# Two rows of the last tile stored so that one DMA engine gets less: half by SyncE, half by GpSimd on 15 engines

## The chip, the cores and the metric

The kernel runs on one core of a Trainium2 chip. The metric is the time of one execution in microseconds (us). All runs here are in the fast state or, where a run stands alone, of unknown state, with a granted clock of 1.0 in each. The effects are below 0.1%, so runs are compared only with runs of the kernel before from the same chip.

## The reference

```python
z = x + residual                                   # 32 x 2048 rows of 2048 float32
rms = np.sqrt(np.mean(z ** 2, axis=-1, keepdims=True) + eps)
return (z / rms * gamma).astype(np.float32)
```

Two arrays of 537 MB are read and one is written. There is nothing to reuse.

## The kernel before

The rows are cut into tiles of 128 partitions with 7 rows each (the first two tiles are smaller). SyncE loads x and stores the result, ScalarE issues the loads of the residual and computes the sums of squares, VectorE adds and scales in place in the buffer `z`. The last tile is handled in four pieces of 2, 2, 2 and 1 rows, so that its stores can start early:

```python
tail = [(0, 2), (2, 4), (4, 6), (6, 7)]
...
# SyncE, after the stores of all other tiles
for k, (a, b) in enumerate(tail):
    sp.wait_ge(tail_ev["done"], k + 1)             # VectorE has scaled piece k
    sp.dma_start(
        out=rows(o_f, last)[:, a:b, :], in_=z[last % 2][:, a:b, :]
    ).then_inc(s_tail, U)                          # U = 16: one increment per DMA engine
...
# GpSimd takes no part but for the waits at the end
nc.gpsimd.wait_ge(s_tail, U * len(tail))
nc.gpsimd.sem_clear(range(ids[0], ids[-1] + 1))
```

One row of one partition is 8 KB, so one row of a tile is 1 MB. In the trace the four stores of the tail land 16 times each (64 landings), with 384 packets of 16 KB and 128 of 8 KB. Dealt alike to the 16 DMA engines this is 8 partitions of each store, 24 packets of 611 ns and 8 of 309 ns, 17.1 us of work.

Of the kernel before, what the change touches and what calls it, by code (L numbers as in the profile page):

```python
# [9 lines left out]
def kernel(  # L10
# [5 lines left out]
    eps: float,  # L16
    out: bass.AP,
):



# [6 lines left out]
    nc = tc.nc  # L28
    P = nc.NUM_PARTITIONS
# [4 lines left out]
    x_f = x.flatten_outer_dims()  # L34
    r_f = residual.flatten_outer_dims()
    o_f = out.flatten_outer_dims()
# [4 lines left out]
    U = 16  # L41
# [8 lines left out]
    last = n_tiles - 1  # L50

    LO = 3
    n_iter = (last - LO) // 2
    HI = LO + 2 * n_iter
    assert n_iter >= 1

    def rows(t, i):
        k = sizes[i]
        return t[starts[i] : starts[i] + P * k, :].rearrange("(p r) m -> p r m", r=k)
# [5 lines left out]
    def sb(name, shape):  # L65
        return ctx.enter_context(nc.sbuf_tensor(name, shape, fp32))
# [6 lines left out]
    def sem(name):  # L73
        sems.append(ctx.enter_context(nc.semaphore(name)))
        return sems[-1]
# [3 lines left out]
    z = [sb(f"z{p}", [P, R, D]) for p in range(2)]  # L79
# [2 lines left out]
    ssq = [[sb(f"ssq{p}{h}", [P, 4]) for h in range(2)] for p in range(2)]  # L82
    rms = [[sb(f"rms{p}{h}", [P, 4]) for h in range(2)] for p in range(2)]
    rstd = [[sb(f"rstd{p}{h}", [P, 4]) for h in range(2)] for p in range(2)]
    tail_ssq = sb("tail_ssq", [P, R])
    tail_rms = sb("tail_rms", [P, R])
    tail_rstd = sb("tail_rstd", [P, R])
# [8 lines left out]
    dve = sem("dve_own")  # L96
    act = sem("act_own")
    s_tail = sem("s_tail")
    tail_ev = {k: sem(f"tail_{k}") for k in ("add", "rms", "done")}


    tail = [(0, 2), (2, 4), (4, 6), (6, 7)]
# [30 lines left out]
    def load_x(sp, t, d=0):  # L133
        i = t.i + d
        inc(sp.dma_start(out=z[i % 2][:, : sizes[i], :], in_=rows(x_f, i)), "x_in", i)

    def load_r(sp, t, d=0):
        i = t.i + d
        e = entry(i)
        inc(  # L140
            sp.dma_start(  # L141
                out=r_area[:, e : e + sizes[i], :],
                in_=rows(r_f, i) if t.it is None else r_full[t.it + (i - 2)],
            ),
            "r_in",
            i,
        )

    def sp_turn(sp, t):
        i = t.i  # L150
        t.wait(sp, "done", -1)
        inc(
            sp.dma_start(out=rows(o_f, i - 1), in_=z[(i - 1) % 2][:, : sizes[i - 1], :]),
            "s_out",
            i - 1,
        )
        if i == last:
            return
        t.wait(sp, "s_out", -1)
        if i + 1 == last:  # L160
            for k, (a, b) in enumerate(tail):
                sp.dma_start(  # L162
                    out=z[last % 2][:, a:b, :], in_=rows(x_f, last)[:, a:b, :]
                ).then_inc(x_tail[k], U)
        else:
            load_x(sp, t, 1)
# [50 lines left out]
    def act_part(s, chain, src, a, b, sq, rm):  # L217

        for g in range(a, b):
            if g > a:  # L220
                chain.wait()
            chain.next(
                s.activation(  # L223
                    out=sq_junk[:, :],
                    in_=src[:, g, :],
                    func=Act.Square,
                    accum_out=sq[:, g - a : g - a + 1],
                )
            )
        chain.wait()  # L230
        return s.activation(  # L231
            out=rm, in_=sq[:, : b - a], func=Act.Sqrt, bias=eps_tile[:, :], scale=inv_d
        )

    def act_turn(s, t, chain):
        i, p = t.i, t.p
        for h, (a, b) in enumerate(parts(i)):
            chain.wait()
            t.wait(s, "add_a" if h == 0 else "add_b")
            if h == 0 and i > 0:  # L240
                load_r(s, t, 1)
            inc(
                act_part(s, chain, z[p], a, b, ssq[p][h], rms[p][h][:, : b - a]),
                "rms_a" if h == 0 else "rms_b",
                i,
            )
# [6 lines left out]
    def sync_program(sp):  # L253
        load_x(sp, Turn(0))
        load_r(sp, Turn(0))

        sp.wait_ge(tail_ev["add"], 1)
        for q in range(4):
            sp.dma_start(  # L259
                out=stage[32 * q : 32 * q + 1],  # L260
                in_=gamma.partition_broadcast(1).rearrange("p (a b) -> p a b", a=16),
            ).then_inc(g_in, U)
        load_r(sp, Turn(1))
        load_x(sp, Turn(1))
        for i in range(1, n_tiles):
            sp_turn(sp, Turn(i))
        for k, (a, b) in enumerate(tail):
            sp.wait_ge(tail_ev["done"], k + 1)
            sp.dma_start(
                out=rows(o_f, last)[:, a:b, :], in_=z[last % 2][:, a:b, :]  # L270
            ).then_inc(s_tail, U)

    def vector_program(v):
        v.memset(eps_tile[:, :], float(eps))  # L274
        v.memset(stage, 0.0).then_inc(tail_ev["add"], 1)  # L275
        v.wait_ge(g_in, 4 * U)
        v.stream_shuffle(gamma_tile[:, :].rearrange("p (a b) -> p a b", a=16), stage, [0] * 32)  # L277
        for i in range(LO):
            dve_turn(v, Turn(i), lambda i, h: (2 * i + h + 1) * U)
        with v.Fori(0, 2 * n_iter, 2) as it:  # L280
            for i in range(LO, LO + 2):
                dve_turn(v, Turn(i, it), lambda i, h: it * (2 * U) + (2 * i + h + 1) * U)
        for i in range(HI, last):
            dve_turn(v, Turn(i), lambda i, h: (2 * i + h + 1) * U)
        base = 2 * last * U
        t = Turn(last)
        t.wait(v, "r_in")

        def tail_scale(k):
            a, b = tail[k]  # L290
            v.wait_ge(tail_ev["rms"], k + 1)
            v.reciprocal(out=tail_rstd[:, a:b], in_=tail_rms[:, a:b]).then_inc(dve, U)  # L292
            v.wait_ge(dve, base + (k + 1) * U)
            scale(v, last, a, b, tail_rstd, a).then_inc(tail_ev["done"], 1)

        for k, (a, b) in enumerate(tail):
            v.wait_ge(x_tail[k], U)
            add(v, last, a, b).then_inc(tail_ev["add"], 1)
            if k:
                tail_scale(k - 1)  # L300
        tail_scale(len(tail) - 1)

    def scalar_program(s):
        chain = Chain(s, act)
        for i in range(LO):
            act_turn(s, Turn(i), chain)
        with s.Fori(0, 2 * (n_iter - 1), 2) as it:
            n = chain.n
            chain.base = it * R
            for i in range(LO, LO + 2):  # L310
                act_turn(s, Turn(i, it), chain)
            assert chain.n - n == 2 * R
        chain.base = None
        chain.n = n + 2 * R * (n_iter - 1)
        for i in range(HI - 2, last):
            act_turn(s, Turn(i), chain)
        for k, (a, b) in enumerate(tail):
            chain.wait()
            s.wait_ge(tail_ev["add"], k + 2)
            act_part(  # L320
                s, chain, z[last % 2], a, b, tail_ssq[:, a:b], tail_rms[:, a:b]
            ).then_inc(tail_ev["rms"], 1)

    sync_program(nc.sync)
    vector_program(nc.vector)
    scalar_program(nc.scalar)

    nc.gpsimd.wait_ge(ev["s_out"][(last - 1) % 2], ((last - 1) // 2 + 1) * U)
    nc.gpsimd.wait_ge(s_tail, U * len(tail))
    ids = [a.num for a in sems]  # L330
    assert ids == list(range(ids[0], ids[0] + len(ids)))
    nc.gpsimd.sem_clear(range(ids[0], ids[-1] + 1))
# [35 lines left out]
```

## Time and profile before

| | |
|---|---|
| time, median of 4 runs | 3724.88 us (3724.73 to 3724.96) |
| moved | 1610.68 MB at 433 GB/s |
| busy VectorE, ScalarE, GpSimd | 62%, 29%, 0% of the span |
| VectorE's last instruction ends | 3708.8 us |
| last landing of a store | 3722.59 us |

The prediction shows the end of the run in windows. Of the same view, these are the two windows ahead of those; the columns are the window, its length, the busy time of VectorE, ScalarE and GpSimd with their instructions, the granted clock, the mean busy share of the 16 DMA engines, and the rate in GB/s.

```profile
3690.00:3700.00 10.00, 9.96 (x6) 4.42 (x6) 0.00 (x0) 1.00 0.94 406
3700.00:3710.00 10.00, 8.73 (x6) 2.30 (x3) 0.00 (x0) 1.00 0.98 418
```

### The profile page before, as it was taken

How to read it: one execution, taken by the hardware profiler on the slowest of the kernel's cores; microseconds unless marked ns; L12 is line 12 of the kernel's file. 1: busy time of each engine (PE TensorE's matmuls, PEld its weight loads, DVE VectorE, ACT ScalarE, POOL GpSimd, SP SyncE). 2: the span in 40 equal slices, each digit the busy share in tenths (PEclk: the TensorE clock that was granted, in tenths of full speed). 3: DMA queues.
4: the chain of work that ended last, by engine and by line, in shares of the span. 5: the costliest groups of instructions: out<-in, count | busy, mean ns of one | idle time of the engine just before them, and what ended most of it. 6: DMA issues, size and time to landing. Idle time of an engine off the chain costs nothing.

```text
span 3723.7 us, 3798 instructions
## 1 busy us (share of the span) xinstructions
DVE 2302.6 (62%) x816; ACT 1072.4 (29%) x1176; POOL 0.2 (0%) x4
## 2 busy tenths in 40 slices
DVE  5666665566665566665566665566665566665566
ACT  2233322233322233322233322233322233322233
POOL 0000000000000000000000000000000000000000
DMA  9999999999999999999999999999999999999999
GB/s 421 431 434 435 434 434 435 434 435 435 434 434 434 434 434 434 434 434 433 434 434 434 434 434 434 434 434 434 434 434 434 434 434 434 434 434 434 434 432 398
DMA packets 32963, 1610.68 MB, mean 433 GB/s; under 512 B 3712, under 2 KB 3776, under 8 KB 3776
## 3 DMA queue, kind: packets, MB, share of 16 engines
q1 hardware_dynamic: 22592, 1082.17, 67.2%
q10 hardware_dynamic: 10368, 528.49, 32.8%
q14 instruction: 3, 0.02, 0.0%
HBM read 1073.77 MB, written 536.87 MB: 433 GB/s over the span
## 4 chain that ended last, share of the span: by engine, by line
DMA 67%; DVE 22%; issue 9%; ACT 2%; SPq 0%; DVEq 0%; ACTq 0%
DMA out_dram<-z 39%; DMA z<-in_x_dram 27%; DVE z L172 15%; DVE z L177 7%; ACT sq_junk L223 1%; ACT rms L231 0%; DVE rstd L197 0%; SPq L259 0%; DVEq L127 0%; DVE r_area L275 0%; ACTq L211 0%; ACTq L127 0%; SPq L141 0%; DVE tail_rstd L292 0%; SPq L162 0%
## 5 line engine op out<-in xcount | busy, mean ns | idle before, releaser
L172 DVE TENSOR_TENSOR z<-z,r_area 128x8192 f32<-128x8192 f32 (+2 forms) x150 | 1109.5, 7437 | 1252.5 <-DMA z<-in_x_dram 1252.5
L223 ACT ACTIVATE sq_junk<-z 128x2048 f32<-128x2048 f32 x512 | 963.4, 1882 | 2617.1 <-DVE z L172 2605.7
L177 DVE SCALAR_TENSOR_TENSOR z<-z,rstd,gamma_tile 128x2048 f32<-128x2048 f32 x505 | 1153.6, 2344 | 5.2
L197 DVE RECIPROCAL rstd<-rms 128x4 f32<-128x4 f32 (+2 forms) x146 | 25.3, 173 | 130.8 <-ACT rms L231 130.8
L223 ACT ACTIVATION_READ_ACCUMULATOR sq_junk<-z 128x1 f32 x512 | 95.5, 186 | 0.0
L231 ACT ACTIVATE rms<-ssq,eps_tile 128x4 f32<-128x4 f32 (+2 forms) x146 | 43.3, 297 | 13.4
L177 DVE SCALAR_TENSOR_TENSOR z<-z,tail_rstd,gamma_tile 128x2048 f32<-128x2048 f32 x7 | 16.2, 2345 | 0.1
L277 DVE LOAD_MASK_SELECT gamma_tile<-r_area x1 | 0.0, 14 | 16.1 <-DMA r_area<-in_gamma_dram 16.1
L277 DVE STREAM_SHUFFLE gamma_tile<-r_area 128x2048 f32<-128x2048 f32 x1 | 2.3, 2290 | 0.0
L275 DVE MEMSET r_area<- 128x2048 f32 x1 | 1.8, 1765 | 0.4 <-issue 0.4
L223 ACT ACT_TABLE_LOAD x1 | 1.3, 1283 | 0.9 <-SPq L77 0.9
L231 ACT ACT_TABLE_LOAD x1 | 1.3, 1283 | 0.1
L231 ACT ACTIVATE tail_rms<-tail_ssq,eps_tile 128x2 f32<-128x2 f32 (+1 forms) x4 | 1.2, 295 | 0.1
L274 DVE MEMSET eps_tile<- 128x1 f32 x1 | 0.1, 59 | 1.0 <-SPq L77 1.0
L292 DVE RECIPROCAL tail_rstd<-tail_rms 128x2 f32<-128x2 f32 (+1 forms) x4 | 0.6, 158 | 0.0
L349 POOL MEMSET const-bfloat16-1.0<- 128x1 bf16 x1 | 0.1, 101 | 0.0
L349 POOL MEMSET const-uint8-127<- 128x1 uint8 x1 | 0.1, 101 | 0.0
L349 POOL MEMSET const-float32-0.0<- 128x1 f32 x1 | 0.1, 98 | 0.2 <-issue 0.2
L349 POOL MEMSET const-float32-1.0<- 128x1 f32 x1 | 0.1, 98 | 0.0
## 6 DMA issues: line engine op xcount, KB each, us to landing
r_area<-in_residual_dram ACTq DMA_DIRECT2D x72, 7168.0 KB, 35.5
z<-in_x_dram SPq DMA_DIRECT2D x71, 7168.0 KB, 27.5
out_dram<-z SPq DMA_DIRECT2D x71, 7168.0 KB, 40.8
z<-in_x_dram SPq DMA_DIRECT2D x3, 2048.0 KB, 17.9
out_dram<-z SPq DMA_DIRECT2D x3, 2048.0 KB, 15.0
r_area<-in_residual_dram SPq DMA_DIRECT2D x1, 5120.0 KB, 25.0
z<-in_x_dram SPq DMA_DIRECT2D x1, 5120.0 KB, 36.7
out_dram<-z SPq DMA_DIRECT2D x1, 5120.0 KB, 26.5
```

Source lines behind the costliest of these rows:

```text
L172: return v.tensor_add(out=s, in0=s, in1=r_area[:, e + a : e + b, :])
L177: ins = v.scalar_tensor_tensor(out=s, in0=s, scalar=rs[:, c + g - a : c + g - a + 1], in1=gamma_tile[:, :], op0=mult, op1=mult,)
L197: v.reciprocal(out=rstd[p][h][:, :n], in_=rms[p][h][:, :n]).then_inc(dve, U)
L223: s.activation(out=sq_junk[:, :], in_=src[:, g, :], func=Act.Square, accum_out=sq[:, g - a : g - a + 1],)
L231: return s.activation(out=rm, in_=sq[:, : b - a], func=Act.Sqrt, bias=eps_tile[:, :], scale=inv_d)
L274: v.memset(eps_tile[:, :], float(eps))
L275: v.memset(stage, 0.0).then_inc(tail_ev["add"], 1)
L277: v.stream_shuffle(gamma_tile[:, :].rearrange("p (a b) -> p a b", a=16), stage, [0] * 32)
L292: v.reciprocal(out=tail_rstd[:, a:b], in_=tail_rms[:, a:b]).then_inc(dve, U)
L349: nc = _bacc.Bacc("TRN2", target_bir_lowering=False, num_devices=1)
```

## The change

The intent is to take work from one DMA engine in the last tile. It is called the fifth, because f1 finds it in a probe load of 5 partitions and not in one of 4; the four engines of the probe of 4 are called the first four. Rows 1 and 3 leave the full stores. SyncE stores their even partitions (64), GpSimd 60 of the odd ones, and SyncE the last 4. Two tiny loads on GpSimd, of 5 and of 12 partitions, stand before and behind its store.

```diff
-        for k, (a, b) in enumerate(tail):
+        for k, (a, b) in enumerate([(0, 1), (2, 3), (4, 6), (6, 7)]):
             sp.wait_ge(tail_ev["done"], k + 1)
-            sp.dma_start(
-                out=rows(o_f, last)[:, a:b, :], in_=z[last % 2][:, a:b, :]
-            ).then_inc(s_tail, U)
+            store_last(sp, slice(0, P), slice(a, b)).then_inc(s_tail, U)
+            if k == 1:
+                store_last(sp, slice(0, P, 2), slice(1, 4, 2)).then_inc(s_tail, U)
+                store_last(sp, slice(121, P, 2), slice(1, 4, 2)).then_inc(s_tail, U)
...
+    def pool_program(g):
...
+        turn(5, 0)                                  # tiny load of 5 partitions
+        g.wait_ge(tail_ev["done"], 2)
+        store_last(g, slice(1, 120, 2), slice(1, 4, 2)).then_inc(soft[2], U)
+        turn(12, 16)                                # tiny load of 12 partitions
+        for k in soft:
+            g.wait_ge(k, U)
+        g.dma_reset(range(soft[0].num, soft[-1].num + 1))
```

More of the change, by code (lines that the diff above doesn't have):

```diff
@@ L54 @@
     HI = LO + 2 * n_iter
-    assert n_iter >= 1
+    assert n_iter >= 1 and P == 128
     def rows(t, i):
@@ L84 @@
     rstd = [[sb(f"rstd{p}{h}", [P, 4]) for h in range(2)] for p in range(2)]
+    tiny = sb("tiny", [12, 32])
     tail_ssq = sb("tail_ssq", [P, R])
@@ L98 @@
     s_tail = sem("s_tail")
+    soft = [sem(f"soft{k}") for k in range(3)]
     tail_ev = {k: sem(f"tail_{k}") for k in ("add", "rms", "done")}
@@ L266, in sync_program, with store_last, turn, two_pairs @@
             sp_turn(sp, Turn(i))
-        for k, (a, b) in enumerate(tail):
+        for k, (a, b) in enumerate([(0, 1), (2, 3), (4, 6), (6, 7)]):
             sp.wait_ge(tail_ev["done"], k + 1)
-            sp.dma_start(
-                out=rows(o_f, last)[:, a:b, :], in_=z[last % 2][:, a:b, :]
-            ).then_inc(s_tail, U)
+            store_last(sp, slice(0, P), slice(a, b)).then_inc(s_tail, U)
+            if k == 1:
+                store_last(sp, slice(0, P, 2), slice(1, 4, 2)).then_inc(s_tail, U)
+                store_last(sp, slice(121, P, 2), slice(1, 4, 2)).then_inc(s_tail, U)
+    n_tail = 4 + 2
+    def store_last(eng, q, r):
+        return eng.dma_start(out=rows(o_f, last)[q, r, :], in_=z[last % 2][q, r, :])
+    def pool_program(g):
+        def turn(k, c):
+            def two_pairs(t):
+                return t[:k, c : c + 16].rearrange("p (a b) -> p a b", a=2)[:, :, :2]
+            g.dma_start(out=two_pairs(tiny), in_=two_pairs(x_f)).then_inc(soft[c // 16], U)
+        turn(5, 0)
[5 more added lines that the diff above has]
+        g.dma_reset(range(soft[0].num, soft[-1].num + 1))
     def vector_program(v):
@@ L326 @@
     scalar_program(nc.scalar)
+    pool_program(nc.gpsimd)
     nc.gpsimd.wait_ge(ev["s_out"][(last - 1) % 2], ((last - 1) // 2 + 1) * U)
-    nc.gpsimd.wait_ge(s_tail, U * len(tail))
+    nc.gpsimd.wait_ge(s_tail, U * n_tail)
     ids = [a.num for a in sems]
```

## The prediction

Passages of the recorded text that no trace or run of this case shows are cut, and the cuts marked: on what grounds a store runs on which engines, and the ground of rival 2, that the stores of the tail would run at a lower rate, with its worst case.

> **What bounds the kernel now.** I read the page first. VectorE is busy 62% and ScalarE 29% of the span, and no row of the page says that either of them is what the program waits for: the DMA row stands at 9 from the first slice to the last.
>
> ```profile
> span 3723.7 us, 3798 instructions
> DVE 2302.6 (62%) x816; ACT 1072.4 (29%) x1176; POOL 0.2 (0%) x4
> DMA  9999999999999999999999999999999999999999
> q1 hardware_dynamic: 22592, 1082.17, 67.2%
> q10 hardware_dynamic: 10368, 528.49, 32.8%
> HBM read 1073.77 MB, written 536.87 MB: 433 GB/s over the span
> ```
>
> The two queue shares add up to 100% of sixteen engines' time. The time is bytes over rate, 1610.68 MB at 433 GB/s, and the change moves no byte less. So nothing can be gained except where the sixteen engines are not all busy. The second view cuts the end of the run into windows; its last two columns are the mean busy share of the 16 DMA engines and the rate.
>
> ```profile
> 3710.00:3716.00 6.00, 0.00 (x0) 0.00 (x0) 0.00 (x0) 1.00 0.98 421
> 3716.00:3717.00 1.00, 0.00 (x0) 0.00 (x0) 0.00 (x0) 1.00 0.82 344
> 3717.00:3718.00 1.00, 0.00 (x0) 0.00 (x0) 0.00 (x0) 1.00 0.37 156
> 3718.00:3719.00 1.00, 0.00 (x0) 0.00 (x0) 0.00 (x0) 1.00 0.18 74
> 3719.00:3720.00 1.00, 0.00 (x0) 0.00 (x0) 0.00 (x0) 1.00 0.08 33
> 3720.00:3721.00 1.00, 0.00 (x0) 0.00 (x0) 0.00 (x0) 1.00 0.06 25
> 3721.00:3722.00 1.00, 0.00 (x0) 0.00 (x0) 0.00 (x0) 1.00 0.06 25
> ```
>
> A share of 0.06 is 1/16: from about 3719.7 us on a single engine is still storing. The raw landing times of the last store, one increment per engine, say the same: eleven engines at 3716.9 to 3717.9, four at 3718.8 to 3719.3, one at 3722.59; the span ends 1.15 us later. That straggler is also last in every earlier store of this tile, and its lag has grown over the run: the last load of the first part of the run spreads over 1 us, the late ones over 5 and more. It is one slow engine, not an accident of the tail.
>
> The third view is the timeline of the tail, with its column of the DMA-issuing queue (SPq). The four stores of the last tile are issued long before they land:
>
> ```profile
> 3690.41 18.76 SPq L269 DMA_DIRECT2D out_dram<-z  x4
> 3706.46 2.35 DVE L177 SCALAR_TENSOR_TENSOR z<-z,tail_rstd,gamma_tile 128x2048 f32<-128x2048 f32 x1
> ...
> out_dram<-z SPq DMA_DIRECT2D x3, 2048.0 KB, 15.0
> out_dram<-z SPq DMA_DIRECT2D x1, 1024.0 KB, 13.8
> ```
>
> A 2 MB store needs 4.8 us at 434 GB/s and takes 15 us to land, so it waits some 10 us behind older work in the engines' queues. VectorE ends at 3708.8 us, 14 us ahead of the last landing. In this tail neither computing nor issuing counts, only how many bytes each single engine still has to move.
>
> [...] Nothing in the kernel before uses GpSimd for a DMA or stores a part of the partitions[...].
>
> **The change part by part.** [...] So the diff wants the fifth engine relieved, and I take it that the author knows it to be the straggler. The kernel's trace names no engine; this is the assumption that I cannot check.
>
> Bytes per engine of the last tile: one row of 128 partitions is 8 partitions x 8 KB = 64 KB on each engine, seven rows 448 KB. Afterwards:
> - fifth engine: rows 0 and 2, 128 KB; its 4 of the 64 even partitions, rows 1 and 3, 64 KB; rows 4 and 5, 128 KB; row 6, 64 KB: 384 KB.
> - first four: 448 KB by the same sum with GpSimd's 4 partitions (64 KB), plus one of the partitions 121 to 127 each, two rows, 16 KB: 464 KB.
> - the other eleven: 448 KB.
>
> 384 + 4 x 464 + 11 x 448 = 7168 KB, the whole tile. Each engine moves 434 / 16 = 27.1 GB/s. The fifth loses 64 KB, 65,536 B / 27.1 GB/s = 2.42 us: landing at 3722.59 - 2.42 = 3720.2. In packets (309 ns for 8 KB, 611 ns for 16 KB in the trace) it is 24 x 611 + 8 x 309 before against 8 x 611 + 32 x 309 after, 2.36 us less. The first four gain 16 KB, 0.6 us; if they are the four that are late already, 3719.3 + 0.6 = 3719.9, still ahead of 3720.2. So the whole 2.4 us shows in the end.
>
> Costs: SyncE issues row 2, then two more stores at about 0.35 us each (the page's stores from L269 take 332 to 344 ns), after "done" at 3699.4. The engines then still hold older work: row 0 alone lasts until about 3702.4 (the first store landed at 3704.8, less the 2.4 us of the row that it no longer carries). The new stores have about 3 us to arrive, so I expect no gap. GpSimd's two 8-byte loads carry no bytes worth counting. Its reset waits for its own three transfers, which should land near 3711, 9 us ahead of the end. Three more semaphores are cleared in one range instruction. Sum: -2.4 us, with +0.5 us that I choose for packets of two queues, the finer pieces[...]: about -1.9.
>
> **The rivals.**
> 1. The relief goes to the wrong engine: [...] the straggler is not the fifth. Then it keeps its 448 KB and the end stays: 3724.9; with 464 KB, 3725.5. For it: [...] nothing here shows which engine lags. [...] About one in five.
> 2. [...] I expect a part of a microsecond; one in six that it eats the gain.
> 3. GpSimd's path becomes a new wait: slow descriptors, a late reset, or more work at start and end of the program for a third queue. Its slack of 9 us speaks against the first two; for the third I leave up to 1 us.
> 4. The main loop changes. No instruction in it does, and the 40 slices say that it is bound by bytes: excluded but for chance.
>
> **Range and chances.** Perfect levelling bounds the gain: the shares after 3716 us add up to 0.82 + 0.37 + 0.18 + 0.08 + 0.06 + 0.06 = 1.57 us of all sixteen, so the packets could end at 3717.6 instead of 3722.1, a gain of 4.5 us or 0.12% at the very most. Two per cent would be 74 us; neither side of it is within reach. Central value: 3724.93 - 1.9 = 3723.0. Low end: 3721.9, the full 2.4 and some luck at the ends. High end: 3725.8, rival 1 or a mild rival 2. The three runs before lie within 0.23 us, so the scatter does not widen this.
>
> **What the changed profile would show.** Right: a third queue with about 1 MB (60 x 2 x 8 KB = 983 KB), the last landing near 3720.2, the window 3721 to 3722 empty, four engines at about 3719 to 3720 and the span near 3721.5. Rival 1: the last two windows still at 0.06 until 3722. Rival 2: a DMA share or rate well under 0.98 and 420 GB/s between 3702 and 3712, with the bulk of the landings behind 3718. Rival 3: GpSimd's wait or reset ending after the last landing. The prediction is wrong if the end is above 3725.8, most likely by rival 2, or if a gap opens near 3702 because the smaller first store leaves the engines without work before the new ones arrive.

## More of the kernel before

A share counts how long packets were under way, the rate counts what they carried.

A packet is counted whole in the window in which it starts, so a share can pass 1.

## The result, and the profile after

| | median | runs |
|---|---|---|
| before | 3724.88 us | 3724.73 to 3724.96 (4) |
| changed | 3724.22 us | 3725.25, 3724.12, 3724.31, 3723.87 |

The ratio is 0.9999, with a 95% interval of 0.9981 to 1.0016. Ratios here are the mean time of one kernel's fast runs over that of the other's of the same rounds, so not quite the ratio of the medians. The interval is wider than anything that this change can do. The medians differ by 0.66 us. The profiled run, 3725.25, is the slowest of the four; the other three lie below all four runs before.

The queues and issues of the changed kernel, from its page and from the view of its DMA issues (queue: packets, MB, share; then size and us from issue to landing):

```profile
q0 software_dynamic: 208, 0.98, 0.1%
...
out_dram<-z POOLq DMA_DIRECT2D x1, 960.0 KB, 12.0
```

GpSimd's store is there as planned. GpSimd's timeline (start, duration, in us) shows that issuing it takes 0.65 us, and the store then has until the end of the run.

```profile
3700.45 0.65 POOL L282 DMA_DIRECT2D out_dram<-z  x1 [3698.18 <-DVE z L182]
3701.09 0.56 POOL L290 DMA_DIRECT2D tiny<-in_x_dram  x1
```

The windows of the changed kernel's end, to be set beside those of before:

```profile
3690.00:3700.00 10.00, 9.96 (x5) 5.10 (x8) 0.00 (x0) 1.00 0.96 414
3700.00:3710.00 10.00, 9.44 (x7) 2.30 (x3) 1.21 (x2) 1.00 0.98 353
3710.00:3716.00 6.00, 0.00 (x0) 0.00 (x0) 0.00 (x0) 1.00 1.00 395
3716.00:3717.00 1.00, 0.00 (x0) 0.00 (x0) 0.00 (x0) 1.00 1.03 434
3717.00:3718.00 1.00, 0.00 (x0) 0.00 (x0) 0.00 (x0) 1.00 0.91 385
3718.00:3719.00 1.00, 0.00 (x0) 0.00 (x0) 0.00 (x0) 1.00 0.53 221
3719.00:3720.00 1.00, 0.00 (x0) 0.00 (x0) 0.00 (x0) 1.00 0.33 139
3720.00:3721.00 1.00, 0.00 (x0) 0.00 (x0) 0.00 (x0) 1.00 0.25 106
3721.00:3722.00 1.00, 0.00 (x0) 0.00 (x0) 0.00 (x0) 1.00 0.08 33
```

Two things have changed. Between 3700 and 3710 us the share is 0.98 as before, but the rate is 353 GB/s where it was 418. That is 65 GB/s x 10 us = 0.65 MB not moved; the next six microseconds lose another (421 - 395) x 6 = 0.16 MB. Together, at 434 GB/s, this is 1.9 us of all 16 engines. And the end is no longer one engine alone: in the window from 3720 a share of 0.25 says that four are still at work, where it was 0.06 before. The last landing is at 3722.30 us.

The packet records say what the lost rate is. Before, every 8 KB packet of the tail takes 309 ns and none is longer. In the changed kernel the 120 packets of GpSimd's store take 411 ns in the mean and up to 1319, and SyncE's 8 KB packets 340 in the mean and up to 1431. I call this **stretch**: the time of each packet after 3690 us, less the shortest of its size and queue, summed. It is 30 us in this trace, which over 16 engines is again 1.9 us.

### The profile page after: what moved, and what is told of

Same layout as the page of the kernel before. It is cut to its first block, busy times and chain, and to the rows that moved or that the text cites. A ratio compares the mean times of both kernels' runs of the same rounds, so it can differ in the third digit from the quotient of the medians.

```text
span 3723.5 us, 3805 instructions
## 1 busy us (share of the span) xinstructions
DVE 2302.6 (62%) x816; ACT 1072.4 (29%) x1176; POOL 2.1 (0%) x7
## 4 chain that ended last, share of the span: by engine, by line
DMA 67%; DVE 22%; issue 9%; ACT 2%; SPq 0%; DVEq 0%; ACTq 0%
DMA out_dram<-z 39%; DMA z<-in_x_dram 27%; DVE z L177 15%; DVE z L182 7%; ACT sq_junk L228 1%; ACT rms L236 0%; DVE rstd L202 0%; SPq L264 0%; DVEq L132 0%; DVE r_area L302 0%; ACTq L216 0%; ACTq L132 0%; SPq L146 0%; DVE tail_rstd L319 0%; SPq L167 0%
## 5 line engine op out<-in xcount | busy, mean ns | idle before, releaser
L236 ACT ACTIVATE rms<-ssq,eps_tile 128x4 f32<-128x4 f32 (+2 forms) x146 | 43.3, 297 | 13.4
```

Source lines behind the costliest of these rows:

```text
L236: return s.activation(out=rm, in_=sq[:, : b - a], func=Act.Sqrt, bias=eps_tile[:, :], scale=inv_d)
```

## The experiments

Twelve kernels ran. In each group the kernel before ran on the same chip. Stretch is read from the packet records as above. All outputs were correct.

| run | median us (runs) | before, same chip | rate 3700 to 3710 | stretch, us |
|---|---|---|---|---|
| e1 halves by SyncE | 3724.97 (3724.75 to 3725.33) | 3724.97 | 416 | 0 |
| e2 full rows by SyncE | 3724.91 (3724.65 to 3725.10) | 3724.97 | 424 | 0 |
| e3 other engine left out | 3725.19 (3724.96 to 3725.46) | 3724.97 | 394 | 16 |
| e4 one row dealt anew | 3726.10 (3725.19 to 3726.37) | 3724.97 | 370 | 20 |
| f1 probes, before | 3725.19 (one) | 3725.25 | 426 | 0 |
| f2 probes, changed | 3724.72 (one) | 3725.25 | 369 | 23 |
| f3 full rows by GpSimd | 3725.23 (3724.89 to 3725.75) | 3725.25 | 423 | 0 |
| f4 half by GpSimd on 16 engines | 3725.02 (3724.97 to 3725.03) | 3725.25 | 424 | 0 |
| g1 odd partitions rotated | 3724.67 (3723.89 to 3726.27) | 3725.26 | 379 | 15 |
| g2 changed kernel again | 3724.67 (3724.43 to 3725.74) | 3725.26 | 385 | 13 |
| g3 tiny loads behind the store | 3725.66 (3725.55 to 3726.51) | 3725.26 | 385 | 15 |
| h1 row 0 in 19 stores | 3726.14 (3725.97 to 3726.81) | 3725.11 | 366 | 23 |

The kernel before ranged from 3724.63 to 3726.11 us over these four groups, within each group by 0.6 to 1.3 us. Differences of medians below half a microsecond are therefore not told as findings; the rate and the stretch are much clearer signs than the time.

**e1: are half stores the loss?** GpSimd is taken out. Theory A, in this and the next expectations, puts the loss on stores that deal a part of the partitions.

```diff
-                store_last(sp, slice(121, P, 2), slice(1, 4, 2)).then_inc(s_tail, U)
+                store_last(sp, slice(1, P, 2), slice(1, 4, 2)).then_inc(s_tail, U)
...
-    pool_program(nc.gpsimd)
```

> GpSimd is out of it: SyncE stores rows 1 and 3 as two halves, the 64 even partitions and then the 64 odd ones, over all 16 engines, so every engine has the 448 KB of the kernel before. Theory A [...]: the loss of the changed kernel stays without its relief, so 1.5 to 2.5 us slower than before, 3726.4 to 3727.4 us, and the rate between 3700 and 3710 us falls from 418 to some 350 GB/s as in the changed kernel. Theory B (the loss comes from GpSimd's third queue): 3724.9, rate 418. Theory C (the loss comes from finer pieces or from the smaller first store): 3725.5 to 3726.5, and the next run shows the same.

The rate stays and so does the time:

```profile
3700.00:3710.00 10.00, 7.86 (x6) 2.30 (x3) 0.00 (x0) 1.00 0.98 416
```

Theory A in this form is refuted: half stores through SyncE cost nothing here, 3724.97 us beside 3724.97. Every 8 KB packet takes 309 ns.

**e2: are small, late pieces or GpSimd's tiny loads the loss?**

```diff
-                store_last(sp, slice(0, P, 2), slice(1, 4, 2)).then_inc(s_tail, U)
-                store_last(sp, slice(121, P, 2), slice(1, 4, 2)).then_inc(s_tail, U)
+                store_last(sp, slice(0, P), slice(1, 4, 2)).then_inc(s_tail, U)
...
-        store_last(g, slice(1, 120, 2), slice(1, 4, 2)).then_inc(soft[2], U)
-        turn(12, 16)
+        turn(11, 16)
```

> Rows 1 and 3 are stored by SyncE for all 128 partitions in one store, so the pieces are as small (8 KB) and come as late as in the changed kernel, and GpSimd keeps its two tiny loads and its reset, but stores nothing. Theory A: [...] as before, 3724.6 to 3725.2 us and a rate near 418 between 3700 and 3710. Theory C or a cost of GpSimd's tiny loads and reset: 3725.5 or more.

3724.91 beside 3724.97, no stretch. The 8 KB pieces, the smaller first store, the tiny loads and the reset of GpSimd's state are all free here. No gap opened near 3702 us.

**e3: does it matter which engine is left out?**

```diff
-        turn(5, 0)
+        turn(12, 0)
...
-        turn(12, 16)
+        turn(5, 16)
```

> The two tiny loads change places, 12 partitions first and 5 last[...]. If [...] the fifth engine is the straggler, it loses its relief of 2.4 us and the time rises by that against the changed kernel: 3726.0 to 3727.0 us, with a single engine at a share of 0.06 for the last 2 us. If the relief of the fifth has no effect, 3724.2 as in the changed kernel[...].

3725.19, against 3724.97 before. The rise over the changed kernel was forecast as 1.8 us or more and is 1.0 against the first median and 0.5 against its second, and on other chips, so the size missed. The shape is near the expected one: one or two engines are left from 3719 us on, where the changed kernel had four from 3720 us on.

```profile
3719.00:3720.00 1.00, 0.00 (x0) 0.00 (x0) 0.00 (x0) 1.00 0.14 57
3720.00:3721.00 1.00, 0.00 (x0) 0.00 (x0) 0.00 (x0) 1.00 0.08 33
3721.00:3722.00 1.00, 0.00 (x0) 0.00 (x0) 0.00 (x0) 1.00 0.02 8
```

**e4: half of the bytes dealt anew.** GpSimd stores 120 partitions of row 0, SyncE the other 8 in two stores of 4.

```diff
-        for k, (a, b) in enumerate([(0, 1), (2, 3), (4, 6), (6, 7)]):
+        for k, (a, b) in enumerate([(1, 2), (2, 4), (4, 6), (6, 7)]):
...
-                store_last(sp, slice(0, P, 2), slice(1, 4, 2)).then_inc(s_tail, U)
-                store_last(sp, slice(121, P, 2), slice(1, 4, 2)).then_inc(s_tail, U)
+                store_last(sp, slice(120, 124), slice(0, 1)).then_inc(s_tail, U)
+                store_last(sp, slice(124, 128), slice(0, 1)).then_inc(s_tail, U)
...
-        g.wait_ge(tail_ev["done"], 2)
-        store_last(g, slice(1, 120, 2), slice(1, 4, 2)).then_inc(soft[2], U)
+        g.wait_ge(tail_ev["done"], 1)
+        store_last(g, slice(0, 120), slice(0, 1)).then_inc(soft[2], U)
```

The condition ahead of SyncE's two small stores also becomes `k == 0`.

> The same relief with half of the bytes dealt anew: only row 0 is taken out of the full stores, [...] rows 1 to 6 are full stores. Bytes per engine are as in the changed kernel (384, 464, 448 KB). Theory A: loss about in proportion to the bytes dealt anew, half of 1.8 us, so 3724.9 - 2.4 + 0.9 = 3723.4 us (3722.9 to 3723.9). Theory B or C: nothing gained over the changed kernel, 3724 to 3725.

A miss: 3726.10, slower than before in the median, with 20 us of stretch for half of the bytes. So the loss does not go by the bytes dealt anew. This store is issued 9 us earlier, while the previous tile's 56 KB packets are still in the queues, and four of those stretch too, one to 3.03 us where they take 2.12. The slowest engine lands the previous tile's store at 3707.7 us, in e1, e2 and e3 at 3704.7 to 3705.2.

The packet records show more: this run did not have "the same relief". The slowest engine's last two 56 KB packets, 3701.99 to 3704.11 and 3704.90 to 3707.02 us, have an 8 KB packet of GpSimd's queue between them and another behind, so this engine carried a part of GpSimd's store. The engine left out is one that was done with the previous tile at 3701.70 us. Why the store of 120 partitions was dealt so, no run shows. As a test of the time that theory A forecast, e4 is spoiled; its stretch still counts.

**f1 and f2: which engine is last?** Two tiny loads of 4 and 5 partitions stand behind the last store on SyncE's queue, with semaphores of their own.

```diff
+        for k in (4, 5):
+            sp.dma_start(
+                out=probe[:k, 32 * (k - 4) : 32 * (k - 4) + 16], in_=x_f[:k, :16]
+            ).then_inc(s_probe[k - 4], U)
```

> The kernel before with two probes behind its last store: tiny loads of 4 and of 5 partitions on SyncE, [...] each with its own semaphore, so that their landings tell when those engines have done their stores. If the fifth engine is the straggler, the probe of 5 has four landings before 3720 us and one near 3723, and the probe of 4 has none so late. If another engine lags, all nine landings are early. The time is as before or up to 1 us more.

> The changed kernel with the same two probes. Theory D (the fifth engine is relieved and the first four, which carry 16 KB more and are stretched, now end last): the four landings of the probe of 4 lie at 3721 to 3723 us, the fifth of the probe of 5 near 3720. Theory E (the relief did not reach the straggler): the fifth landing of the probe of 5 is the last of all, near 3722.

The landings of the probes, from the trace's semaphore records, in us (the first record of each probe, soon after its issue at 3709 to 3712 us, is left out):

```
before,  4 partitions: 3716.55 3717.68 3718.70 3719.38
before,  5 partitions: 3716.73 3717.85 3718.87 3719.57 3722.21
changed, 4 partitions: 3718.51 3718.82 3720.49 3721.30
changed, 5 partitions: 3718.69 3719.00 3720.67 3721.48 3721.75
```

The probe of 4 lands four times and that of 5 five times, taken here as one landing on each engine. Four landings of the second follow those of the first by 0.17 to 0.19 us; the last one, 3722.21 before, exists only in the probe of 5. By the names given above, **the fifth engine is the straggler**. Its lag has grown over the run: in f1 the last landing of a load came 0.2 us behind the second last at the start and 2.5 us at the end. Theory D and theory E each hold by half. In the changed kernel the fifth is still last, at 3721.75, but the slowest of the first four has come up to 0.3 us before it: it went from 3719.38 to 3721.30, 1.9 us, of which 16 KB would explain 0.6, if the store of 4 partitions runs on these four. The fifth engine's last stretch of work can be timed from its landing of the previous tile's store: 3704.96 to 3722.02 before, 17.06 us, and 3705.28 to 3721.55 with the change, 16.27. It moved 64 KB less, 2.4 us, and was faster by 0.8. By the packet times of the trace its work should take 17.1 us before, as it does, and 8 x 611 + 32 x 309 ns = 14.8 us with the change. So the fifth engine itself lost 1.5 us of its relief, and it began 0.3 us later. (One run of each kernel.)

**f3 and f4: is it GpSimd's queue?** In f3 GpSimd stores rows 1 and 3 of all partitions, in f4 the odd half on 16 engines. Theory A2 puts the stretch on GpSimd's store of 60 partitions, and theory B on any store through GpSimd's queue.

```diff
-        store_last(g, slice(1, 120, 2), slice(1, 4, 2)).then_inc(soft[2], U)
+        store_last(g, slice(0, P), slice(1, 4, 2)).then_inc(soft[0], U)       # f3
+        store_last(g, slice(1, P, 2), slice(1, 4, 2)).then_inc(soft[0], U)    # f4
```

In both the tiny loads and the 4-partition store are gone; f3 has no half store of SyncE either.

> GpSimd stores rows 1 and 3 of all 128 partitions in one store on all 16 engines, SyncE the other rows; no relief, no tiny loads. Theory A2 [...]: packets of 8 KB stay at 309 ns, time as before, 3724.7 to 3725.2. Theory B (any store through GpSimd's queue stretches packets, whatever the partitions): means of 365 to 410 ns as in the runs with a GpSimd store so far, time above 3725.5.

> As the run in which SyncE stored both halves, but the 64 odd partitions go through GpSimd, at the same time as the 64 even ones through SyncE, both on 16 engines. Theory A2: if both are dealt to the engines alike, [...] nothing stretches, 309 ns and 3724.7 to 3725.2 us; stretched packets here but not in the run with all 128 partitions would say that GpSimd deals 64 partitions in another way than SyncE. Theory B: stretched, above 3725.5.

The window of f3 and then of f4:

```profile
3700.00:3710.00 10.00, 8.49 (x6) 2.30 (x3) 0.32 (x1) 1.00 1.00 423
```

```profile
3700.00:3710.00 10.00, 8.07 (x6) 2.30 (x3) 0.00 (x0) 1.00 1.00 424
```

No packet is stretched in either. The stores through GpSimd's queue that run on all 16 engines cost nothing here, even beside one of SyncE's: 3725.23 us (f3) and 3725.02 (f4) beside 3725.25. Theory B is refuted.

**g1, g2, g3: is it the tiny load ahead of the store, or the split of the odd partitions?** g2 is the changed kernel again. g3 puts the tiny loads behind the store. g1 splits the odd partitions in another way: GpSimd stores the last 44, SyncE the first 20 in five stores of 4.

```diff
 # g1
-                store_last(sp, slice(121, P, 2), slice(1, 4, 2)).then_inc(s_tail, U)
+                for m in range(4):
+                    store_last(sp, slice(1 + 2 * m, 32, 8), slice(1, 4, 2)).then_inc(s_tail, U)
+                store_last(sp, slice(33, 40, 2), slice(1, 4, 2)).then_inc(s_tail, U)
...
-        store_last(g, slice(1, 120, 2), slice(1, 4, 2)).then_inc(soft[2], U)
-        turn(12, 16)
+        store_last(g, slice(41, P, 2), slice(1, 4, 2)).then_inc(soft[1], U)
```

```diff
 # g3
-        turn(5, 0)
         g.wait_ge(tail_ev["done"], 2)
         store_last(g, slice(1, 120, 2), slice(1, 4, 2)).then_inc(soft[2], U)
+        turn(5, 0)
         turn(12, 16)
```

> The same relief of the fifth engine (384, 464 and 448 KB as in the changed kernel), but the odd partitions of rows 1 and 3 are dealt[...]: GpSimd stores partitions 41 to 127, 44 in number[...], and SyncE stores the other 20 in five stores of 4 partitions[...]. Theory A2 [...]: packets of 8 KB stay near 309 ns, the fifth engine needs 2.4 us less from its previous landing to its last (14.7 in place of 17.1 us), the time is about 2 us below before, 3722.5 to 3723.3. Theory F (15 or fewer engines through GpSimd stretch in any case[...]): stretched as in the changed kernel, 3724 to 3725.

> The changed kernel again, unchanged, on the chip of these runs: 0.3 to 1.0 us below before, with 20 to 30 us of stretch summed over its 8 KB packets. It gives the scatter of the changed kernel beside the others.

> The changed kernel with both tiny loads behind the store[...]; no relief for the fifth. Theory A2: [...] no stretch (309 ns), and the time is that of before, within 0.4 us. Theory F: stretched as in the changed kernel, and as the fifth has its full 448 KB, 1 to 2 us above before.

Theory A2 forecast packets of 309 ns for g1 and g3. It misses in both: g3, without a tiny load ahead of the store, has 15 us of stretch, and g1 is stretched by 15 us and as fast as the changed kernel. Which engine takes which partitions, on which A2 rested, no run shows. The three windows, g1, g2 and g3:

```profile
3700.00:3710.00 10.00, 7.99 (x6) 2.30 (x3) 0.00 (x0) 1.00 0.96 379
```

```profile
3700.00:3710.00 10.00, 8.04 (x6) 2.30 (x3) 0.27 (x1) 1.00 0.97 385
```

```profile
3700.00:3710.00 10.00, 8.57 (x6) 2.30 (x3) 1.47 (x3) 1.00 0.98 385
```

g2 has less stretch than expected, 13 us. Its median lies 0.6 us below before, as in the first group (0.7) and in f2 (0.5, one run). g3 beside g2 is the cleanest measure of the relief: the same stores and stretch within 2 us, one with the fifth engine left out and one without. The medians are 3724.67 and 3725.66, **1.0 us for the relief**. All four runs of g3 lie above all nine of before, but its median is only 0.4 us higher, less than is told as a finding here.

**h1: row 0 in 19 stores.** Row 0 is cut into ten stores of SyncE and nine of GpSimd. Theory G forecast that this cut would avoid the stretch; its ground, an assumed dealing of partitions to engines, is not shown by any run.

```diff
-        for k, (a, b) in enumerate([(0, 1), (2, 3), (4, 6), (6, 7)]):
+        for k, (a, b) in enumerate([(1, 2), (2, 4), (4, 6), (6, 7)]):
...
+            if k == 0:
+                for m in range(4):
+                    store_last(sp, slice(m, 16, 4), slice(0, 1)).then_inc(s_tail, U)
+                    store_last(sp, slice(32 + m, 48, 4), slice(0, 1)).then_inc(s_tail, U)
+                store_last(sp, slice(16, 20), slice(0, 1)).then_inc(s_tail, U)
+                store_last(sp, slice(48, 52), slice(0, 1)).then_inc(s_tail, U)
...
+        store_last(g, slice(52, 96), slice(0, 1)).then_inc(soft[5], U)
+        for m in range(4):
+            turn(5, 16 * (m + 1))
+            store_last(g, slice(20 + m, 32, 4), slice(0, 1)).then_inc(soft[6 + 2 * m], U)
+            store_last(g, slice(96 + m, P, 4), slice(0, 1)).then_inc(soft[7 + 2 * m], U)
```

> The same relief (384 KB on the fifth engine, 464 on the first four, 448 on the others), by row 0 alone, cut into stores[...]. Theory G [...]: stretch summed over the packets under 3 us (13 to 30 us in the changed kernel), the fifth engine needs 14.7 us from its previous landing to its last, the time is 1.8 to 2.4 us below before. Theory F (stores on fewer than 16 engines through GpSimd stretch packets[...]): 10 us of stretch or more, and a time like that of the run that dealt row 0 in order, at or above before.

A clear miss for theory G: 3726.14, all five runs above all nine of before, and 23 us of stretch. Theory F's forecast came true: 10 us or more, and a time like e4's 3726.10. But h1 issues its row as early as e4 and in 19 stores, so more than the dealing differs from the changed kernel. GpSimd's own packets are hardly stretched (2.6 us in 88), but SyncE's of 8 and 16 KB are, by 8 and 11 us. At the end some five engines are left, not one:

```profile
3720.00:3721.00 1.00, 0.00 (x0) 0.00 (x0) 0.00 (x0) 1.00 0.29 123
3721.00:3722.00 1.00, 0.00 (x0) 0.00 (x0) 0.00 (x0) 1.00 0.33 139
```

**What is shown and what stays open.** Stretch, 13 to 30 us, is present in all eight traces with large stores on fewer than 16 engines (the changed kernel and e3, e4, f2, g1, g2, g3, h1), with rates of 353 to 394 GB/s between 3700 and 3710 us; it is absent in all six whose large stores run on 16 (before, e1, e2, f1, f3, f4), with 416 to 426. Neither GpSimd's queue (f3, f4), nor half stores (e1), nor 8 KB pieces (e2), nor the tiny load ahead of the store (g3) is its cause alone. Every stretched run has both a GpSimd store of fewer than 128 partitions that leaves out an engine and a SyncE store of 4 partitions, so which of the two stretches the packets was not taken apart. The stretch is not confined to the time of GpSimd's packets: in the changed kernel 4.9 of its 30 us, in g1 4.8 of 15, fall on SyncE packets that start after GpSimd's last has ended. What lengthens the packets stays open: no run shows it, and g1 and h1 were built on an assumed dealing of partitions to engines that no run shows either. None of the versions beats the changed kernel.

Which engine was left out can be read from the packet records. GpSimd's queue carries 4-byte packets: 16 with a store on all 16 engines (f3, f4), 24 with the store of 60 partitions (40 less the 16 of the tiny load behind it, which e2 shows alone), so 8 more, as many as each other engine has of 8 KB. In the changed kernel, f2, g1 and g2 the slowest engine's last 56 KB packet is followed at once (within 25 ns) by such a 4-byte packet, at 3705.77 us in the changed kernel; in e3 and g3 it is followed by an 8 KB packet of GpSimd's store. I read this as: the slowest engine was left out in the former, as meant, and was not in the latter. In h1, too, it was left out.

## Why the prediction was right or wrong

- **What bounds the kernel, and the ceiling on the gain**: right. The change moved the time by 0.66 us, far inside the stated 4.5. That the median lies in the range says little for the mechanism: the kernel before, 3724.88, lies in it as well.
- **The fifth engine is the straggler**: assumed there, borne out by f1: 3722.21 us against 3716.73 to 3719.57 for the four before it.
- **GpSimd's store leaves out the fifth**: right for this store. The trace names no engine, but the 4-byte packets show that GpSimd's store left out one engine and that it was the slowest; with the tiny loads the other way round (e3) or behind the store (g3) it was not. With g3 and g2 the order of the tiny loads alone moves the median by 1.0 us. So rival 1 did not come true here; it did in e4.
- **"The fifth loses 64 KB ... 2.42 us"**: the bytes are right, the time is not. It gained 0.8 us in f2, because it needed 1.5 us more than the 14.8 of its packets unstretched. "So the whole 2.4 us shows in the end" is the step that failed.
- **"The first four gain 16 KB, 0.6 us ... 3719.9"**: this failed with it. The slowest of them ended 1.9 us later and nearly became the last.
- **"+0.5 us that I choose for packets of two queues, the finer pieces"**: this is the term that was mis-sized. In f2 the fifth engine lost 1.5 us against its packet times and 0.3 to its later start, 1.8 in place of 0.5. That is 1.3 us more, about the 1.4 by which f2's gain (0.5 us, one run) falls short of the 1.9 of the prediction. Over all engines, the stretch is 1.9 us in the profiled run, the slowest of its four, and 0.8 us in g2 (13.4 / 16). Of the term's named causes, two queues and finer pieces cost nothing (f4 3725.02 us beside 3725.25, e2 3724.91 beside 3724.97, no stretch in either). What the stretched runs have in common, stores on fewer engines beside full ones, was not thought of.
- **Rival 2** spoke of a rate "well under 0.98 and 420 GB/s" as its sign. The sign came, in the rate and not in the share, and 19 landings of the tail's stores lie behind 3718 us, where before there were 6. The size is 1.9 us. The reason that it gave is cut, as no run shows it; it was given one chance in six to eat the gain, and the loss ate most of it.
- **Rival 3**: refuted. GpSimd's transfers had landed by 3713.2 us, 2 us later than expected but 9 us before the last store; the span ends 1.16 us after the last landing, before 1.15; and e2 shows no cost. (The tiny loads are of 16 bytes per partition, 80 and 192 bytes in all, and not of 8 bytes; it makes no difference.)
- **A gap near 3702**: did not open.
- The expected signs "last landing near 3720.2", "window 3721 to 3722 empty" and "span near 3721.5" failed: 3722.30, 0.08 and 3723.5 in the profiled run, the slowest of the four; in g2, whose profiled run is its median, the last landing is at 3721.73 and the span 3722.9. The range held the median because its high end allowed for a spoiled relief. It also said that scatter would not widen it; the changed kernel's own runs spread over 1.4 us where before's four spread over 0.23. (The prediction's 3724.93 is the median of the three runs that it knew; a fourth made it 3724.88.)

## What to carry to other kernels

When a run is bound by DMA bytes, look at its last microseconds by single engines: a share of 0.06, 1/16, meant one engine still at work here, and probe loads of 4 and of 5 partitions behind the last store told that it was the one that the probe of 5 had and that of 4 had not (f1: 3722.21 us against 3719.57 for the latest of the others). Before shifting work between engines, put the rate beside the busy share: between 3700 and 3710 us the engines of the changed kernel were as busy as before, 0.98, and carried 353 GB/s in place of 418. Here stores on all 16 engines cost nothing whichever queue they used (e1, e2, f3, f4: medians 0 to 0.23 us below before on the same chip, and no stretch), and rearrangements with fewer engines gave back most of what they gained (f2: 1.5 of 2.4 us on the fifth engine, and 0.3 by a later start). Check in the packet records which engine a store leaves out, as e4 left out another than it meant to.
